# A hybrid encoder trunk: the rms factor applied late, D's heads rotated together, and two projections moved between scores

## The chip, the cores and the metric

The kernel runs on one core of one Trainium2 chip. The metric is device time in microseconds of that core. The core has TensorE (PE; its weight loads are shown as PEld), VectorE (DVE), ScalarE (ACT), GpSimd (POOL) and SyncE (SP), which issues the DMAs. Each engine runs its own list of instructions in order and waits on semaphores for the others.

## The reference

Two layers, each with three residual sub-layers, on 512 tokens of width 1024: a mixer of four parallel head groups, an attention to 256 memory tokens, and a dense squared-ReLU MLP. Queries and keys of every group are normalised per head by their root mean square; D's are then rotated.

```python
def rms(x, g):
    y = xf * lax.rsqrt(jnp.mean(xf * xf, axis=-1, keepdims=True) + EPS)
    return (y * g.astype(F32)).astype(x.dtype)

def axial_gqa(q, k, v, g_qk, row, col):          # group D; A, B and C likewise, with other heads and biases
    q = axial_rope(rms(q, g_qk[0]), row, col)
    k = axial_rope(rms(k, g_qk[1]), row, col)
    ...
        p = jax.nn.softmax(sc, axis=-1)

def memory_xattn(h, mem_n, w_xq, w_xkv, g_qk, w_xo):
    q = rms((h @ w_xq).reshape(b, s, X_HEADS, X_DH), g_qk[0])
    kv = (mem_n @ w_xkv).reshape(b, m, 2, X_HEADS, X_DH)
    ...
    return o.reshape(b, s, X_HEADS * X_DH) @ w_xo
```

The rms factor is one number per token and head. A gain is one number per channel, and a rotation mixes channels of one head, so the factor may be multiplied in before or after both.

## The kernel before

All 512 tokens stay on the chip; weights are streamed. Every product is made of float32r matmuls on a high and a low part: `mm3` (L176 to 180) issues three matmuls on the same PSUM tile, high x high (L177), and the two mixed ones (L178, L179). A weight tile is loaded by SP into `wst` (3 buffers), ACT casts it to the high part `whi` (L299, 4 buffers), and POOL subtracts to get the low part `wlo` in four pieces (L167 in `sub_lo`, 4 buffers).

The mixer runs twelve units, B 0 to 3, A 0 to 3, C 0 and 1, D 0 and 1. While the attention of one unit runs, the front of the next is computed: `front_A`, `front_G` (for C and D) and `front_B`. A front projects four token blocks of 128 (`tok_proj`), ACT copies and squares each result and DVE sums the squares (L415, into `sf`). Then `half(j)` works on two token blocks at a time: POOL adds epsilon and takes the power -1/2 (`rpow`, L311 and L312; in `front_B` L716 to 718), DVE multiplies queries and keys by that factor (L452, L552, L722), then by the gains (L454, L557, L725) and, in B and D, rotates them (`rope`, L584, L586, L587). ACT casts the high part and DVE subtracts for the low part (both into `spl`, 2 buffers), and PE transposes them (L403, into PSUM `dn`, 2 buffers), after which the copies `T` (L172 on ACT, L174 on DVE) feed the scores. In D, `rope` is called once for the four query heads and once for the key head; its scratch tile `zr` holds 512 columns, and each call makes four products of 16 columns per head, a product with the cosines and an addition.

Gate and branch products (`gate_piece`, `branch_piece`, PSUM `df`, one buffer) fill PE between the steps of the attentions, by the hand-written string `FILL`.

In the attention to the memory (`xattn`) a token block is projected (24 matmuls of 512 columns into `dn`) and normalised by `xnorm_split`; `q_trans(pr)` transposes the two blocks of pair `pr`, `attend(pr)` makes scores (PSUM `sc`, 2 buffers), softmax (L931 to L936), transposes (L941) and value products for two pairs of heads in turn, and `out_proj(pr)` multiplies by the output weights. The order in the code is projections 0 and 1, projections 2 and 3, `q_trans(0)`, `attend(0)` with `q_trans(1)` before its second half, `attend(1)`, `out_proj(0)`, `out_proj(1)`.

The order of each engine's instructions is made when the kernel is built: a list scheduler simulates the engines and issues, among the instructions whose inputs are there, the one that stands first in the program; `tc.high_priority()` puts an instruction ahead of the others. On the chip that order is fixed.

Of the kernel before, what the change touches and what calls it, by code (L numbers as in the profile page):

```python
# [11 lines left out]
F32R = mybir.dt.float32r  # L12
# [4 lines left out]
P = 128  # L17
# [76 lines left out]
def kernel(  # L94
# [214 lines left out]
    def rpow(dst, src, add, n):  # L309

        G.tensor_scalar(dst, src, add, None, op0=ALU.add)  # L311
        G.tensor_tensor(out=dst, in0=dst, in1=mhalf[:, :n], op=ALU.pow)  # L312

# [117 lines left out]
    def front_A(l, norm, h):  # L431
# [15 lines left out]
        def half(j):  # L447
# [3 lines left out]
            qq, kk = qk[:, :, 0:2, :], qk[:, :, 2:4, :]  # L451
            V.tensor_tensor(out=qk, in0=qk, in1=bc(s.rearrange("p (t h) -> p t h", t=2), 3, 64), op=ALU.mult)  # L452
            for m in range(2):
                V.tensor_tensor(out=kk[:, :, m], in0=kk[:, :, m], in1=bc(ga, 1, 2), op=ALU.mult)  # L454
            sq_ = tl("spl", [P, 2, 2, 2, 64], F32R)
            sk = tl("spl", [P, 2, 2, 2, 2, 64], F32R)
# [76 lines left out]
    def front_G(l, norm, br, g):  # L533
# [14 lines left out]
        def half(j):  # L548
            tk, s = toks[j], st[j]
            rpow(s, s, 64 * EPS, 10)  # L550
            qk = tk[:, :, :320].rearrange("p t (h d) -> p t h d", h=5)
            V.tensor_tensor(out=qk, in0=qk, in1=bc(s.rearrange("p (t h) -> p t h", t=2), 3, 64), op=ALU.mult)  # L552
            kk = qk[:, :, 4, :]
            if br == "C":
                V.tensor_tensor(out=kk, in0=kk, in1=bc(gc, 1, 2), op=ALU.mult)
            else:
                V.tensor_tensor(out=qk, in0=qk, in1=bc(gd, 1, 2), op=ALU.mult)  # L557
                rope(qk[:, :, 0:4], dt_, j, 4, 2)
                rope(qk[:, :, 4:5], dt_, j, 1, 2)
            sq_ = tl("spl", [P, 2, 4, 2, 64], F32R)  # L560
# [15 lines left out]
    def rope(x, tab, j, nh, nax):  # L576

        w = nax * 32
        b2 = slice(2 * j, 2 * j + 2)
        tmp = tl("zr", [P, S])[:, :2 * nh * w].rearrange("p (t h d) -> p t h d", t=2, h=nh)  # L580
# [111 lines left out]
    def front_B(l, cT, p):  # L692
# [20 lines left out]
        for j in range(2):  # L713
            tk, s = toks[j]
            s3 = s.rearrange("p (t c) -> p t c", t=2)
            G.tensor_scalar(s3[:, :, 0:4], s3[:, :, 0:4], 64 * EPS, None, op0=ALU.add)  # L716
            G.tensor_scalar(s3[:, :, 4:6], s3[:, :, 4:6], 32 * EPS, None, op0=ALU.add)
            G.tensor_tensor(out=s, in0=s, in1=mhalf[:, :12], op=ALU.pow)
            qr = tk[:, :, 0:64].rearrange("p t (h d) -> p t h d", h=2)
            qk = tk[:, :, 64:320].rearrange("p t (h d) -> p t h d", h=4)  # L720
            qn, kn = qk[:, :, 0:2], qk[:, :, 2:4]
            V.tensor_tensor(out=qk, in0=qk, in1=bc(s3[:, :, 0:4], 3, 64), op=ALU.mult)  # L722
            V.tensor_tensor(out=qr, in0=qr, in1=bc(s3[:, :, 4:6], 3, 32), op=ALU.mult)
            for h in range(2):
                V.tensor_tensor(out=kn[:, :, h], in0=kn[:, :, h], in1=bc(gbn, 1, 2), op=ALU.mult)  # L725
            for t_ in range(2):
                V.tensor_tensor(out=qr[:, t_], in0=qr[:, t_], in1=bc(gqr, 1, 2), op=ALU.mult)
            rope(qr, bt_, j, 2, 1)
            sq_ = tl("spl", [P, 2, 2, 2, 96], F32R)
            sk = tl("spl", [P, 2, 2, 2, 96], F32R)  # L730
# [89 lines left out]
    def mem_prep(l):  # L820
# [3 lines left out]
        for c in range(2):  # L824
            st = tl("wst", [P, 4, NM])
            SY.dma_start(st, memT[c * 512:(c + 1) * 512, :].rearrange("(k p) t -> p k t", p=P))
            for k in range(4):
# [8 lines left out]
                else:  # L836
                    q = tl("zr", [P, S])[:, :NM]
                    A.activation(q, st[:, k, :], AF.Square)
# [60 lines left out]
    def xattn(l, norm, KT, VX, X, nm):  # L899
# [6 lines left out]

        def proj(pr):
            tok_proj(norm, views, S, ev, tbs=(2 * pr, 2 * pr + 1))

# [6 lines left out]

        def attend(pr):
            for hp in range(2):
                if hp == 1 and pr == 0:
                    q_trans(1)  # L920
                pth = tl("pt", [P, 2, 2, 256], F32R)
                ptl = tl("pt", [P, 2, 2, 256], F32R)
                for qi in range(2):
                    Tq = Tqs[2 * pr + qi]
                    ps = psum("sc").rearrange("p (h k) -> p h k", h=2)
                    for i in range(2):
                        h = 2 * hp + i
                        hs = slice(h * P, (h + 1) * P)
                        mm3(ps[:, i], Tq[:, 0, hs], Tq[:, 1, hs], KT[0][:, h, :], KT[1][:, h, :], True, True)
                    st = stat(6)  # L930
                    V.tensor_reduce(out=st[:, 0:2], in_=ps, axis=AX.X, op=ALU.max, negate=True)  # L931
                    e = ptile()[:, :S].rearrange("p (h k) -> p h k", h=2)
                    for i in range(2):
                        A.activation(e[:, i], ps[:, i], AF.Exp, bias=st[:, i:i + 1], accum_out=st[:, 2 + i:3 + i])
                    V.reciprocal(st[:, 4:6], st[:, 2:4])
                    V.tensor_tensor(out=e, in0=e, in1=bc(st[:, 4:6], 2, NM), op=ALU.mult)  # L936
                    qs = slice(qi * P, qi * P + P)
                    pt = psum("tr")
                    for i in range(2):
                        for kb in range(2):  # L940
                            T.transpose(pt[:, (2 * i + kb) * P:(2 * i + kb + 1) * P], e[:, i, kb * P:(kb + 1) * P], idf)  # L941
                    pv_ = pt.rearrange("p (k q) -> p k q", k=4)
                    hi = pth[:, :, :, qs].rearrange("p h k q -> p (h k) q")
                    lo = ptl[:, :, :, qs].rearrange("p h k q -> p (h k) q")
                    A.copy(hi, pv_)
                    V.tensor_tensor(out=lo, in0=pv_, in1=f(hi), op=ALU.subtract)
                po = psum("pv").rearrange("p (h q) -> p h q", h=2)
                for i in range(2):
                    h = 2 * hp + i
                    for kb in range(2):  # L950
                        hs = slice(h * P, (h + 1) * P)
                        mm3(po[:, i], VX[0][:, kb, hs], VX[1][:, kb, hs], pth[:, i, kb, :], ptl[:, i, kb, :], kb == 0,
                            kb == 1)
                for i in range(2):
                    h = 2 * hp + i
                    ds_ = slice(pr * 256, pr * 256 + 256)
                    A.copy(xo[h][:, 0, ds_], po[:, i])
                    V.tensor_tensor(out=xo[h][:, 1, ds_], in0=po[:, i], in1=f(xo[h][:, 0, ds_]), op=ALU.subtract)

# [15 lines left out]

        proj(0)
        proj(1)
        q_trans(0)
        attend(0)
        attend(1)  # L980
        out_proj(0)
# [294 lines left out]
```

## Time and profile before

| | |
|---|---|
| median of 3 runs | 2363.65 us (2363.37 to 2367.36) |
| the profiled execution | 2361.96 us, of which the span from first to last instruction is 2360.0 us |
| mean granted PE clock | 0.992 of 2.4 GHz |
| busy, share of the span | PE 97%, DVE 59%, POOL 55%, ACT 49% |
| chain of work that ended last | PE 83%, DVE 11%, POOL 2% |

The share of busy time says which engine is nearest to its limit; the waits say which engine made another idle, and for how long in total, how often and at most; the timeline says what ran at a given moment. Ends of matmuls are modelled by the profiler, so they overlap a little.

### The profile page before, as it was taken

The numbers are of one execution on the slowest core, as the hardware profiler recorded it, in microseconds if no ns is written. First come the engines' busy times: TensorE is split into PE (matmuls) and PEld (weight loads), VectorE is DVE, ScalarE is ACT, GpSimd is POOL, SyncE is SP. The second block draws the span as 40 slices with busy tenths as digits, with TensorE's granted clock in tenths as the row PEclk, the third lists the DMA queues.
The fourth block names the chain that finished last, engine by engine and source line by source line (L and its number), as shares of the span: only waits on it lengthen the run. The fifth ranks groups of instructions, "written<-read, shape, count | busy, mean of one in ns | idle before, by whom it ended". The sixth has DMA issues, their size and how long they took to land.

```text
span 2360.0 us, 33643 instructions
## 1 busy us (share of the span) xinstructions
PE 2281.5 (97%) x12032; PEld 1966.0 (83%) x12032; DVE 1384.1 (59%) x2980; ACT 1151.8 (49%) x2253; POOL 1299.0 (55%) x1657
## 2 busy tenths in 40 slices
PE   8999999998999899999999998999989999999999
PEld 7888889887888888888888887898878878888887
DVE  7778666888975642222457786568879648222222
ACT  4556556655653543223345565566556546322321
POOL 7553544625465376666665435355353754766663
PEclk9999999999999999999999999999999999999999
DMA  5321342442454133333343214324425531323332
GB/s 185 108 94 57 102 138 66 127 154 84 147 179 155 54 99 98 98 92 96 111 134 101 83 46 127 113 79 134 136 92 168 171 131 56 106 91 97 98 93 77
DMA packets 88775, 258.25 MB, mean 109 GB/s; under 512 B 9704, under 2 KB 12392, under 8 KB 88608
## 3 DMA queue, kind: packets, MB, share of 16 engines
q1 hardware_dynamic: 88608, 256.10, 34.4%
q8 instruction: 95, 1.56, 0.3%
q14 instruction: 72, 0.59, 0.1%
HBM read 222.46 MB, written 33.60 MB: 109 GB/s over the span
## 4 chain that ended last, share of the span: by engine, by line
PE 83%; DVE 11%; POOL 2%; issue 1%; ACT 1%; DMA 1%; SPq 0%; POOLq 0%; ACTq 0%; DVEq 0%
PE dn L177 13%; PE dn L178 13%; PE dn L179 13%; PE df L177 10%; PE df L179 9%; PE df L178 9%; PE tr L476 3%; PE sc L177 1%; PE sc L179 1%; PE sc L178 1%; PE dn L403 1%; POOL wlo L167 1%; DVE pt L480 1%; DVE zr L584 1%; PE sc L624 1%
## 5 line engine op out<-in xcount | busy, mean ns | idle before, releaser
L167 POOL TENSOR_TENSOR wlo<-wst,whi 128x256 fp32r<-128x256 f32 (+3 forms) x1400 | 1071.0, 797 | 745.4 <-ACT whi L299 671.3
L299 ACT CAST whi<-wst 128x1024 fp32r<-128x1024 f32 (+3 forms) x350 | 348.8, 1003 | 640.8 <-PE dn L178 293.7
L177 PE MATMUL df<-s,whi 128*128 128x512 f32 (+1 forms) x967 | 381.0, 394 | 8.1 <-DVE zg L785 3.2
L179 PE MATMUL df<-s,wlo 128*128 128x512 f32 (+1 forms) x967 | 376.1, 389 | 1.3 <-POOL wlo L167 1.3
L178 PE MATMUL df<-s,whi 128*128 128x512 f32 (+1 forms) x967 | 374.3, 387 | 1.6 <-DVE s L167 1.6
L177 PE MATMUL dn<-whi,s 128*128 128x384 f32 (+4 forms) x768 | 264.8, 348 | 13.6 <-ACT s L348 7.7
L179 PE MATMUL dn<-whi,s 128*128 128x384 f32 (+4 forms) x768 | 263.3, 343 | 0.0
L178 PE MATMUL dn<-wlo,s 128*128 128x384 f32 (+4 forms) x768 | 263.1, 344 | 0.0
L177 PEld LDWEIGHTS df<-s,whi 128*128 128x128 f32 x967 | 181.7, 188 | 46.6 <-DVE yl L808 6.1
L179 PEld LDWEIGHTS df<-s,wlo 128*128 128x128 f32 x967 | 181.8, 188 | 38.4 <-POOL wlo L167 2.9
L178 PEld LDWEIGHTS df<-s,whi 128*128 128x128 f32 x967 | 181.9, 188 | 34.3 <-DVE s L167 2.2
L178 PE MATMUL dn<-s,whi 128*128 128x512 f32 (+1 forms) x529 | 197.1, 373 | 0.0
L179 PE MATMUL dn<-s,wlo 128*128 128x512 f32 (+1 forms) x529 | 196.9, 373 | 0.0
L177 PE MATMUL dn<-s,whi 128*128 128x512 f32 (+1 forms) x529 | 196.5, 374 | 0.0
L177 PEld LDWEIGHTS dn<-whi,s 128*128 128x128 f32 x768 | 146.8, 192 | 24.5 <-ACT s L348 7.7
L480 DVE TENSOR_TENSOR pt<-tr,pt 128x512 fp32r<-128x512 f32 (+1 forms) x224 | 142.7, 644 | 26.0 <-ACT pt L479 17.3
L178 PEld LDWEIGHTS dn<-wlo,s 128*128 128x128 f32 x768 | 147.2, 192 | 8.9 <-POOL wlo L167 0.2
L179 PEld LDWEIGHTS dn<-whi,s 128*128 128x128 f32 x768 | 146.8, 191 | 6.9
L479 ACT CAST pt<-tr 128x512 fp32r<-128x512 f32 (+1 forms) x224 | 121.8, 556 | 55.9 <-PE tr L476 54.3
L311 POOL TENSOR_SCALAR sf<-sf 128x8 f32<-128x8 f32 (+2 forms) x44 | 13.9, 316 | 241.3 <-DVE sf L415 239.5
L179 PEld LDWEIGHTS dn<-s,wlo 128*128 128x128 f32 x529 | 99.6, 188 | 17.9 <-POOL wlo L167 0.2
L178 PEld LDWEIGHTS dn<-s,whi 128*128 128x128 f32 x529 | 99.6, 188 | 17.8
(376 smaller groups left out, 4827.3 us busy)
## 6 DMA issues: line engine op xcount, KB each, us to landing
wst<-in_wts_dram SPq DMA_DIRECT2D x272, 512.0 KB, 3.5
wst<-in_wts_dram SPq DMA_DIRECT2D x64, 384.0 KB, 3.1
yl<-yz SPq DMA_DIRECT2D x48, 512.0 KB, 4.0
yz<-zg SPq DMA_DIRECT2D x64, 256.0 KB, 2.2
yz<-yl SPq DMA_DIRECT2D x48, 256.0 KB, 3.0
bias<-tscr SPq DMA_DIRECT2D x16, 320.0 KB, 3.3
yl<-yz SPq DMA_DIRECT2D x16, 256.0 KB, 3.1
bias<-tscr SPq DMA_DIRECT2D x8, 448.0 KB, 3.5
```

The costliest lines, as they stand in the source:

```text
L167: (eng or V).tensor_tensor(out=dst, in0=src, in1=f(hi), op=ALU.subtract)
L177: a = T.matmul(ps, lhsT=lh, rhs=rh, start=first, stop=False)
L178: T.matmul(ps, lhsT=lh, rhs=rl, start=False, stop=False)
L179: b = T.matmul(ps, lhsT=ll, rhs=rh, start=False, stop=last)
L299: chain("wh", A.copy(hi[:, :n], st[:, :n]))
L311: G.tensor_scalar(dst, src, add, None, op0=ALU.add)
L403: T.transpose(ps[:rows_, i * P:(i + 1) * P], s, idn)
L476: T.transpose(ps[:, kb * P:(kb + 1) * P], src[:, kb * P:(kb + 1) * P], idn)
L479: A.copy(hi, pv)
L480: V.tensor_tensor(out=lo, in0=pv, in1=f(hi), op=ALU.subtract)
L584: V.tensor_tensor(out=tmp[:, :, :, o:o + 16], in0=x[:, :, :, oo:oo + 16], in1=bc(tab[:, 1, b2, o:o + 16], 2, nh), op=ALU.mult)
L624: T.matmul(ps[:, :nk], lhsT=q, rhs=Tk[:, 0, kb0 * P:kb0 * P + nk], start=True, stop=False)
```

## The change

`rpow` adds epsilon on DVE instead of POOL and gives the power a high priority; `front_B` does the same in its own lines. In `front_A`, `front_G` and `front_B` the multiplication by the factor moves behind the gains and the rotation. In D one call of `rope` rotates five heads, with a scratch tile of 640 columns. In `xattn` projections 2 and 3 move behind the first and the second half of the first pair's attention, one at a time, and use the PSUM buffer `df`; `attend` is split by pairs of heads.

```diff
     def rpow(dst, src, add, n):
-        G.tensor_scalar(dst, src, add, None, op0=ALU.add)
-        G.tensor_tensor(out=dst, in0=dst, in1=mhalf[:, :n], op=ALU.pow)
+        V.tensor_scalar(dst, src, add, None, op0=ALU.add)
+        with tc.high_priority():
+            G.tensor_tensor(out=dst, in0=dst, in1=mhalf[:, :n], op=ALU.pow)
...
             rpow(s, s, 64 * EPS, 8)
-            V.tensor_tensor(out=qk, in0=qk, in1=bc(s.rearrange("p (t h) -> p t h", t=2), 3, 64), op=ALU.mult)
             for m in range(2):
                 V.tensor_tensor(out=kk[:, :, m], in0=kk[:, :, m], in1=bc(ga, 1, 2), op=ALU.mult)
+            V.tensor_tensor(out=qk, in0=qk, in1=bc(s.rearrange("p (t h) -> p t h", t=2), 3, 64), op=ALU.mult)
...
-            rpow(s, s, 64 * EPS, 10)
-            V.tensor_tensor(out=qk, in0=qk, in1=bc(s.rearrange("p (t h) -> p t h", t=2), 3, 64), op=ALU.mult)
             if br == "C":
                 V.tensor_tensor(out=kk, in0=kk, in1=bc(gc, 1, 2), op=ALU.mult)
             else:
                 V.tensor_tensor(out=qk, in0=qk, in1=bc(gd, 1, 2), op=ALU.mult)
-                rope(qk[:, :, 0:4], dt_, j, 4, 2)
-                rope(qk[:, :, 4:5], dt_, j, 1, 2)
+                rope(qk, dt_, j, 5, 2)
+            rpow(s, s, 64 * EPS, 10)
+            V.tensor_tensor(out=qk, in0=qk, in1=bc(s.rearrange("p (t h) -> p t h", t=2), 3, 64), op=ALU.mult)
...
-            G.tensor_scalar(s3[:, :, 0:4], s3[:, :, 0:4], 64 * EPS, None, op0=ALU.add)
-            G.tensor_scalar(s3[:, :, 4:6], s3[:, :, 4:6], 32 * EPS, None, op0=ALU.add)
-            G.tensor_tensor(out=s, in0=s, in1=mhalf[:, :12], op=ALU.pow)
+            V.tensor_scalar(s3[:, :, 0:4], s3[:, :, 0:4], 64 * EPS, None, op0=ALU.add)
+            V.tensor_scalar(s3[:, :, 4:6], s3[:, :, 4:6], 32 * EPS, None, op0=ALU.add)
+            with tc.high_priority():
+                G.tensor_tensor(out=s, in0=s, in1=mhalf[:, :12], op=ALU.pow)
...
-            V.tensor_tensor(out=qk, in0=qk, in1=bc(s3[:, :, 0:4], 3, 64), op=ALU.mult)
-            V.tensor_tensor(out=qr, in0=qr, in1=bc(s3[:, :, 4:6], 3, 32), op=ALU.mult)
...
             rope(qr, bt_, j, 2, 1)
+            V.tensor_tensor(out=qk, in0=qk, in1=bc(s3[:, :, 0:4], 3, 64), op=ALU.mult)
+            V.tensor_tensor(out=qr, in0=qr, in1=bc(s3[:, :, 4:6], 3, 32), op=ALU.mult)
...
-        def proj(pr):
-            tok_proj(norm, views, S, ev, tbs=(2 * pr, 2 * pr + 1))
+        def proj(*tbs):
+            tok_proj(norm, views, S, ev, tbs=tbs, tags=("dn", "dn", "df", "df"))
...
-        proj(0)
-        proj(1)
+
+        proj(0, 1)
         q_trans(0)
-        attend(0)
-        attend(1)
+        attend(0, 0)
+        proj(2)
+        attend(0, 1)
+        proj(3)
+        q_trans(1)
+        attend(1, 0)
+        attend(1, 1)
         out_proj(0)
         out_proj(1)
```

## Rows read from the trace of the kernel before

**Rows 1.** The page, first part: busy us (share of the span) and instructions of each engine.

```profile
PE 2281.5 (97%) x12032; PEld 1966.0 (83%) x12032; DVE 1384.1 (59%) x2980; ACT 1151.8 (49%) x2253; POOL 1299.0 (55%) x1657
```

**Rows 2.** Waits of PE: who waited for whom, us in total, times, longest.

```profile
PE dn L403 <- DVE spl L167: 18.9, 7, 5.4
...
PE sc L177 <- ACT p L934: 6.1, 2, 3.1
PE dn L177 <- DVE sf L415: 4.0, 3, 1.6
...
PE dn L403 <- ACT spl L732: 2.8, 3, 1.1
PE pv L177 <- ACT pt L945: 2.4, 2, 1.2
```

**Rows 3.** Timeline, A, layer 0: start, us, instruction, [idle before <- releaser].

```profile
287.40 0.42 DVE L415 TENSOR_REDUCE sf<-dn 128x4 f32<-128x256 f32 x1 [0.51 <-ACT dn L413]
...
293.20 1.67 POOL L312 TENSOR_TENSOR sf<-sf,mhalf 128x8 f32<-128x8 f32 x1
...
295.07 0.90 DVE L452 TENSOR_TENSOR tok<-tok,sf 128x512 f32<-128x512 f32 x1
...
298.20 0.72 PE L403 MATMUL dn<-jr,spl 128*128 128x128 f32 x4 [3.83 <-DVE spl L167]
```

**Rows 4.** Timeline, D's second half, layer 0.

```profile
537.29 0.47 DVE L415 TENSOR_REDUCE sf<-dn 128x5 f32<-128x320 f32 x1
...
538.46 2.28 POOL L167 TENSOR_TENSOR wlo<-wst,whi 128x192 fp32r<-128x192 f32 x4
540.71 1.98 POOL L312 TENSOR_TENSOR sf<-sf,mhalf 128x10 f32<-128x10 f32 x1
...
542.72 1.22 DVE L552 TENSOR_TENSOR tok<-tok,sf 128x640 f32<-128x640 f32 x1 [1.81 <-POOL sf L312]
...
545.11 1.59 DVE L584 TENSOR_TENSOR zr<-tok,ropd_t 128x128 f32<-128x128 f32 x4
...
549.22 0.84 DVE L584 TENSOR_TENSOR zr<-tok,ropd_t 128x32 f32<-128x32 f32 x4
...
551.65 1.23 PE L403 MATMUL dn<-idr,spl 128*128 128x128 f32 x8 [5.42 <-DVE spl L167]
```

**Rows 5.** Timeline, PE, layer 1: the stalls of A and of D's second half.

```profile
1471.15 0.72 PE L403 MATMUL dn<-jr,spl 128*128 128x128 f32 x4 [3.81 <-DVE spl L167]
...
1724.02 1.23 PE L403 MATMUL dn<-idr,spl 128*128 128x128 f32 x8 [3.88 <-DVE spl L167]
```

**Rows 6.** Windows over six half-clock stretches: length, each engine's busy us, PEclk, DMA; sum.

```profile
549.00:559.20 10.20, 7.04 (x28) 6.82 (x29) 5.17 (x13) 2.48 (x5) 0.70 (x2) 0.50 0.27 83
...
sum 37.40, PE 29.52 PEld 28.44 DVE 23.26 ACT 11.10 POOL 11.43; mean PE 4.92 PEld 4.74 DVE 3.88 ACT 1.85 POOL 1.91
```

**Rows 7.** Timeline, PE, memory attention, layer 0: third projection's start, first transposes.

```profile
773.39 0.50 PE L177 MATMUL dn<-whi,s 128*128 128x512 f32 x1 [1.60 <-DVE sf L415]
...
784.43 0.80 PE L403 MATMUL tr<-idr,spl 128*128 128x128 f32 x8
```

**Rows 8.** Timeline, D's first half, layer 0: a pow on POOL, and DVE.

```profile
521.25 1.99 POOL L312 TENSOR_TENSOR sf<-sf,mhalf 128x10 f32<-128x10 f32 x1
...
521.40 0.67 DVE L167 TENSOR_TENSOR s<-of,s 128x512 fp32r<-128x512 f32 x1
...
525.99 0.82 DVE L557 TENSOR_TENSOR tok<-tok,gd 128x640 f32<-128x640 f32 x1
```

**Rows 9.** Waits of POOL, ACT, DVE and PE around the weight split.

```profile
POOL wlo L167 <- ACT whi L299: 671.3, 219, 29.5
ACT whi L299 <- PE dn L178: 293.7, 82, 4.6
...
DVE tok L722 <- POOL sf L718: 12.5, 6, 2.9
...
PE df L179 <- POOL wlo L167: 1.3, 2, 1.1
```

More of the change, by code (lines that the diff above doesn't have):

```diff
@@ L579, in rope @@
         b2 = slice(2 * j, 2 * j + 2)
-        tmp = tl("zr", [P, S])[:, :2 * nh * w].rearrange("p (t h d) -> p t h d", t=2, h=nh)
+        tmp = tl("zr", [P, 640])[:, :2 * nh * w].rearrange("p (t h d) -> p t h d", t=2, h=nh)
         for ax in range(nax):
@@ L836, in mem_prep @@
                 else:
-                    q = tl("zr", [P, S])[:, :NM]
+                    q = tl("zr", [P, 640])[:, :NM]
                     A.activation(q, st[:, k, :], AF.Square)
@@ L915, in q_trans @@
                 Tqs.append(Tq)
[L917 to L947, printed above, removed]
@@ L948, in attend @@
+        def attend(pr, hp):
+            pth = tl("pt", [P, 2, 2, 256], F32R)
+            ptl = tl("pt", [P, 2, 2, 256], F32R)
+            for qi in range(2):
+                Tq = Tqs[2 * pr + qi]
+                ps = psum("sc").rearrange("p (h k) -> p h k", h=2)
                 for i in range(2):
                     h = 2 * hp + i
-                    for kb in range(2):
-                        hs = slice(h * P, (h + 1) * P)
-                        mm3(po[:, i], VX[0][:, kb, hs], VX[1][:, kb, hs], pth[:, i, kb, :], ptl[:, i, kb, :], kb == 0,
-                            kb == 1)
@@ L954, in attend @@
[L954 to L958, printed above, removed]
+                    hs = slice(h * P, (h + 1) * P)
+                    mm3(ps[:, i], Tq[:, 0, hs], Tq[:, 1, hs], KT[0][:, h, :], KT[1][:, h, :], True, True)
+                st = stat(6)
+                V.tensor_reduce(out=st[:, 0:2], in_=ps, axis=AX.X, op=ALU.max, negate=True)
@@ new lines, in attend @@
+                e = ptile()[:, :S].rearrange("p (h k) -> p h k", h=2)
+                for i in range(2):
+                    A.activation(e[:, i], ps[:, i], AF.Exp, bias=st[:, i:i + 1], accum_out=st[:, 2 + i:3 + i])
+                V.reciprocal(st[:, 4:6], st[:, 2:4])
+                V.tensor_tensor(out=e, in0=e, in1=bc(st[:, 4:6], 2, NM), op=ALU.mult)
+                qs = slice(qi * P, qi * P + P)
+                pt = psum("tr")
+                for i in range(2):
+                    for kb in range(2):
+                        T.transpose(pt[:, (2 * i + kb) * P:(2 * i + kb + 1) * P], e[:, i, kb * P:(kb + 1) * P], idf)
@@ new lines, in attend @@
+                pv_ = pt.rearrange("p (k q) -> p k q", k=4)
+                hi = pth[:, :, :, qs].rearrange("p h k q -> p (h k) q")
+                lo = ptl[:, :, :, qs].rearrange("p h k q -> p (h k) q")
+                A.copy(hi, pv_)
+                V.tensor_tensor(out=lo, in0=pv_, in1=f(hi), op=ALU.subtract)
+            po = psum("pv").rearrange("p (h q) -> p h q", h=2)
+            for i in range(2):
+                h = 2 * hp + i
+                for kb in range(2):
+                    hs = slice(h * P, (h + 1) * P)
+                    mm3(po[:, i], VX[0][:, kb, hs], VX[1][:, kb, hs], pth[:, i, kb, :], ptl[:, i, kb, :], kb == 0,
+                        kb == 1)
@@ L960, in xattn @@
+            for i in range(2):
+                h = 2 * hp + i
+                ds_ = slice(pr * 256, pr * 256 + 256)
+                A.copy(xo[h][:, 0, ds_], po[:, i])
+                V.tensor_tensor(out=xo[h][:, 1, ds_], in0=po[:, i], in1=f(xo[h][:, 0, ds_]), op=ALU.subtract)
         w = []
```

## The prediction

> **What bounds the kernel now.** I read three views in turn. The page's first part says that TensorE (PE) is busy for 97% of the span, with every other engine at 59% or less [rows 1]. So the only time to win is what PE loses: 2360.0 - 2281.5 = 78.5 us of idle time, plus what it works at the lower clock. The list of PE's waits says where the idle time lies [rows 2]: 18.9 us in seven stalls of the fronts' transposes (L403) behind the last subtraction on VectorE (DVE), 2.8 us of the same line behind ScalarE (ACT) in front_B, and in the attention to the memory 6.1 us behind the exponentials (L934) and most of 4.0 us behind the squared sums (L415), which hold PSUM buffers. The rest is scattered over waits that the change does not touch. The timeline then shows what stands behind each stall.
>
> In head group A [rows 3] the squared sums are ready at 287.40 + 0.42 = 287.82, but the pow on GpSimd (POOL) starts at 293.20, behind pieces of the weight split (wlo); DVE can only multiply by the factor at 295.07, and then come the gains (L454), the casts and the subtractions. PE has run dry at 298.20 - 3.83 = 294.37. The second layer repeats it with 3.81 us [rows 5]. In D's second half [rows 4] the sums are ready at 537.76, four wlo pieces go first, the pow ends at 542.69, DVE has idled 1.81 us, and PE stands for 5.42 us until 551.65. In the second layer the same stall is 3.88 us [rows 5].
>
> A long stall costs twice. The stretches of half clock (1.2 of 2.4 GHz) in mid-span are six: the two A stalls, the two D stalls and the two memory attentions, each with such a stall at its start. They last 37.4 us together, and PE is busy for 29.52 us in them [rows 6]. Work at half clock takes twice as long, so 14.8 us are lost, 3.5 of them (half of 7.04) in D of the first layer and 2.3 on average in each of the other five. The Trainium skill (TensorE: Matmul & The Clock Gate, Terms) prices throttled time at the time times one minus the granted ratio, which would be 18.7 us; the rows show that PE is idle for part of it, and the rows decide. By the page the sum below would gain some 3 us more.
>
> **The change, part by part.**
> *A: late factor and early pow.* The add goes to DVE; bounded by nothing and the 0.42 us of the reduce before it, since it writes eight numbers per partition. A high-priority pow waits for at most the piece that is running, 2.28/4 = 0.57 us [rows 4], and takes 1.67 [rows 3]. It is ready by 287.82 + 0.42 + 0.57 + 1.67 = 290.5, while the gains run beside it. The multiplication takes 0.90 us, until 291.4. Between its end in the kernel before (295.97) and PE's start (298.20) lie 2.23 us, some of them gain products that now come earlier; so the transposes are ready by 293.6 at the latest, before PE runs dry at 294.37. Both long stalls go: 3.83 + 3.81 = 7.6 us. Three short ones make up 18.9 - 7.64 - 5.42 - 3.88 = 2.0 us; I take 1.5.
>
> *D: the same, and one rotation in place of two.* Today four q heads and then the k head are rotated separately, with six DVE instructions each; after it there are six for both. Those on 128 elements take 1.59/4 = 0.40 us, those on 32 take 0.84/4 = 0.21 [rows 4], so by a straight line one on 160 takes 0.46. The path from the sums to PE loses 1.81 us of idle time and the 0.84 us of small products, and gets 4 x 0.06 = 0.25 us for the wider products, some 0.5 for two full-width steps at 640 in place of 512 elements (a quarter of 0.82 to 1.22 us each, rows 4 and the quiet one in [rows 8]), and up to 0.4 for the add: 1.5 to 1.9 us shorter. The first half's rotation, which stands ahead on the same queue, is shorter too, by nothing to twice the 0.84 (its products ran beside wlo). So PE's stall of 5.42 falls by 1.5 to 3.6 us, and that of 3.88 as much: I take 3.2 and 3.0 (nearer the upper end, since the first half's six products beside wlo weigh more than those of the second), 6.2 us, and a remainder of 2.2 and 0.9.
>
> *B.* Its 2.8 us are the same chain (reduce, add, pow, multiply, gains, rotation); I take 1.5, bounds 0 and 2.8. The pow also moves past wlo pieces on POOL: 68 pows (48 of front halves, 20 others) go ahead of weight splits. I cost that at nothing, because POOL itself waits 671.3 us for ACT's casts and PE waits for wlo only 1.3 us in all [rows 9]; without that cover each would cost up to its own length.
>
> *Memory attention.* Today all four projections come first: the third waits 1.60 us for a PSUM buffer [rows 7], and after the fourth nothing is left to fill the softmax, so PE stands up to 3.1 and then 1.2 us: with 6.1, 2.4 [rows 2] and twice 1.60 [rows 7] that is 11.7 us in both layers. Now the third goes to the buffer df, which nothing else holds there, so the 1.60 us go. A projection is (784.43 - 773.39)/2 = 5.5 us of PE work; the third covers the normalisation of the first two, the fourth the first softmax. What is late next: df is one buffer, so the fourth must wait until ACT and DVE have emptied the third, two ACT passes and a reduction; and after the fourth the last block's chain must be bridged by the output projection. Bounds for what is left: 0 to the present 5.8 a layer; I take 1.8, which is a stall like the 1.60 and a little. Gain 8.0 us.
>
> *Clock.* If no stall above some 2 us is left in these places, the half clock goes with them: up to 14.8 us. The stall of 1.60 us at 773.39 [rows 7] is followed by none of the six stretches; the stalls that were are 3 us and longer, the shortest of them up to 3.1 [rows 2]. D's remainder of 2.2 us lies between, so I take back 12.5.
>
> **Sum:** 7.6 + 1.5 + 6.2 + 1.5 + 8.0 + 12.5 = 37.3 us. The profiled execution took 2361.96 us (span 2360.0 and 1.96 around it); less 37.3 is 2324.7. It stood 1.7 us below the median of the runs, 2363.65, so the forecast is 2326 us, 1.6% less.
>
> **Does an early pow slow DVE?** In [rows 8] a pow runs from 521.25 to 523.24, and inside it a DVE subtraction with two SBUF inputs takes 0.67 us for 512 elements, 1.31 ns each; with POOL idle the 640-wide product takes 0.82, 1.28 ns each. So it does not, while beside wlo the same width takes 1.22 [rows 4]. The Trainium skill (SBUF — State Buffer, SBUF: two separate sides) says the opposite for this change: a DVE instruction with two SBUF inputs and a GpSimd instruction that reads SBUF exclude each other, and the later one blocks for the whole length of the other. This trace disagrees for the pow; if the page held, the pow would hide under nothing, and that is the third rival.
>
> **The rivals.**
> *1. The memory attention starves.* The query weights stay in their four wlo buffers until the fourth projection, so the output weights (2.28 us on POOL for a tile of 768 columns [rows 4], so 3.0 for one of 1024) come later, and PE finds nothing to fill with. For it: rings of four, and ACT's casts wait 293.7 us for PE to free them. Against: today's fourth projection ends at 784.43, and a shift of some 5 us meets weights that are split at the pace at which two output columns use them. Then 8.0 and some 3 us of clock do not come: 2337; with 5 us of new stalls a layer 2347.
> *2. D stays late.* The casts or PSUM copies are next on its path: 6.2 and 5 us less, 2337; with rival 1 together 2348.
> *3. The pow blocks DVE.* The gains and rotations wait for it, the front's path is as long as before, and only the memory attention and the removal of wlo pieces ahead of the pow are left: some 14 us, 2350. It would be within 0.2% if the attention starves too. Against it stands the row of 0.67 us.
> *4. Slower.* The factor product comes last on DVE's in-order queue. If the pow is held by a wlo piece that waits for ACT's cast, which waits for PE to free a buffer, then DVE stands with everything behind it, among it the subtractions of the running attention, which PE needs. DVE waits today 12.5 us in 6 places for such a pow in front_B [rows 9]. There are 48 front halves; the gains and this balance at 37.3/48 = 0.8 us for each, and at 1.0 us it is 2374. It needs POOL to be late on average; that POOL idles 671.3 us speaks against it.
>
> **Chances.** Forecast 0.60 (own range 2310 to 2338), rival 1 0.14, rival 2 0.11, rival 3 0.07, rival 4 0.08. The low end is all that the touched places lose: 18.9 + 2.8 + 11.7 + 14.8 = 48.2 us, with 4 us for short stalls elsewhere that shift: 2310. The high end takes in both rivals that keep part of the gain, 2348. Left out are rival 4, half of rival 3 and 0.05 of the forecast. A measurement here tells about 0.2%, 4.7 us, from no change. Faster by more: 0.60 + 0.13 + 0.10 + 0.03 = 0.86; within: 0.01 + 0.01 + 0.04 = 0.06; slower 0.08.
>
> **What would show it.** The L403 stalls behind DVE fall from 18.9 to below 5 us; no A stall is left; the pow starts within 1 us of its add; L552 and its like no longer wait for POOL; the D half has one group of 160-wide products; the scores of the memory attention are followed by L177 on df and no stall of 3 us; the granted clock is full from the first microseconds to the last. The forecast is wrong if half-clock stretches stay while the stalls shrink, if new PE waits for wlo appear, or if DVE waits for the pow at its late place.

## The result and the profile after

The changed kernel takes 2340.65 us in the median of four runs (2338.06 to 2346.09), the kernel before on the same chip 2365.51 us (four runs): a ratio of 0.9898 [0.9876, 0.9919], 1.0% less. The profiled execution took 2338.06 us (span 2336.1), against 2361.96: 23.9 us less, where the forecast had taken off 37.3. The sign is right, and the time lies inside the range of 2310 to 2348, though 2.65 us above the 2338 up to which the forecast reckoned by itself: it lies in the part that was added for rivals. 13.4 us of the sum did not come. The question is which of its terms those were.

The page of after, first part, and its list of PE's waits (who waited for whom, us in total, times, longest):

```profile
PE 2273.1 (97%) x12032; PEld 1958.0 (84%) x12032; DVE 1396.7 (60%) x3016; ACT 1145.7 (49%) x2253; POOL 1285.4 (55%) x1573
```

```profile
PE df L177 <- DVE zg L786: 8.5, 12, 2.1
...
PE pv L648 <- DVE pt L481: 4.0, 5, 1.4
...
PE tr L404 <- ACT spl L896: 3.7, 2, 1.9
...
PE sc L177 <- ACT p L932: 1.8, 2, 0.9
...
PE dn L404 <- DVE spl L167: 1.0, 1, 1.0
```

Lines have moved by one to three: L404 is L403 of before, L932 is L934. What led [rows 2] is gone: the transposes' wait for the subtraction on DVE fell from 18.9 us to 1.0, and the scores' wait for the exponentials from 6.1 to 1.8. New are 3.7 us of transposes behind ACT's cast (L896), which is in the attention to the memory, and small waits behind DVE in the mixers.

The windows of before and of after, cut at the first matmul of each query projection and at the start of the next layer, tell which stage gained. Columns: window, length, then busy us of PE, PEld, DVE, ACT and POOL, granted PE clock, DMA share, GB/s. The four rows are the mixer of layer 0, its attention to the memory with the MLP behind it, and the same two of layer 1. Before:

```profile
0.00:759.00 759.00, 722.47 (x4022) 633.67 (x4023) 556.68 (x1279) 429.37 (x897) 395.00 (x525) 0.99 0.39 123
759.00:1196.73 437.73, 430.12 (x2040) 358.31 (x2039) 158.94 (x241) 160.62 (x254) 276.93 (x328) 1.00 0.32 96
1196.73:1926.80 730.07, 706.97 (x3971) 622.91 (x3970) 527.42 (x1237) 415.67 (x873) 368.98 (x493) 0.99 0.36 116
1926.80:2360.00 433.20, 421.94 (x2003) 351.15 (x2001) 141.04 (x223) 146.12 (x232) 258.12 (x313) 0.99 0.28 89
```

After:

```profile
0.00:742.76 742.76, 716.63 (x4022) 629.67 (x4023) 557.05 (x1295) 427.77 (x898) 387.78 (x486) 1.00 0.39 125
742.76:1181.97 439.21, 432.51 (x2041) 359.50 (x2039) 158.25 (x243) 159.46 (x253) 275.17 (x325) 0.99 0.32 96
1181.97:1902.20 720.23, 700.77 (x3970) 617.58 (x3969) 538.62 (x1251) 412.83 (x873) 364.31 (x455) 1.00 0.37 117
1902.20:2336.10 433.90, 423.18 (x2003) 351.27 (x2001) 142.74 (x227) 145.60 (x232) 258.19 (x309) 1.00 0.29 89
```

The mixers became 16.2 and 9.8 us shorter, 26.1 together (unrounded). The attention with the MLP became 1.5 and 0.7 us longer. By this table the fronts gave everything, and the moved projections, on which 8.0 us and a share of the clock had been counted, gave nothing. It compares one execution of each kernel; the first two runs below settle it.

Why they gave nothing stands in the timeline of after, layer 0 (start, us, instruction, [idle before <- releaser]; first ACT's casts and PE's idle time, then the order of PE around them):

```profile
760.23 0.69 ACT L413 ACTIVATE tok<-df,r_x 128x512 f32<-128x512 f32 x1 [1.46 <-PE df L179]
760.82 0.65 ACT L414 ACTIVATE df<-df,r_x 128x512 f32<-128x512 f32 x1
...
761.39 1.27 ACT L896 CAST spl<-tok 128x512 fp32r<-128x512 f32 x2
...
762.06 0.54 PE L404 MATMUL tr<-idr,spl 128*128 128x128 f32 x4 [1.86 <-ACT spl L896]
762.61 0.50 PE L177 MATMUL df<-whi,s 128*128 128x512 f32 x1
...
773.91 0.39 PE L177 MATMUL sc<-T,T 128*128 128x256 f32 x1 [0.91 <-ACT p L932]
775.66 0.63 PE L939 MATMUL tr<-idr,p 128*128 128x128 f32 x4 [0.76 <-DVE p L934]
...
778.36 0.39 PE L177 MATMUL pv<-pt,T 128*128 128x256 f32 x1 [0.68 <-ACT pt L943]
...
780.07 0.38 PE L178 MATMUL pv<-pt,T 128*128 128x256 f32 x1 [1.33 <-DVE pt L944]
```

The third projection (on `df`) was already over at 760.2, before the first transposes: in the built order of PE its matmuls alternate with those of the first two. ACT copies and squares it ahead of the first block's cast, and PE stands 1.86 us. The fourth starts at 762.61, ahead of the scores: 21 of its 24 matmuls precede the first of them. When the softmax comes, nothing is left to fill it, and the stall of up to 3.1 us of before [rows 2], with the shorter one behind it, has become four short ones. The text of the program has the projections between the scores; the order that the list scheduler wrote down has them ahead of them. By the scheduler's rule that is so because `df` was free and their inputs were there; no run tried the same order without `df`.

### The profile page after: what moved, and what is told of

Read it like the earlier page. It is cut to its first block, busy times and chain, and to the rows that moved or that the text cites. A ratio compares the mean times of both kernels' runs of the same rounds, so it can differ in the third digit from the quotient of the medians.

```text
span 2336.1 us, 33596 instructions
## 1 busy us (share of the span) xinstructions
PE 2273.1 (97%) x12032; PEld 1958.0 (84%) x12032; DVE 1396.7 (60%) x3016; ACT 1145.7 (49%) x2253; POOL 1285.4 (55%) x1573
## 3 DMA queue, kind: packets, MB, share of 16 engines
q8 instruction: 95, 1.56, 0.3%
## 4 chain that ended last, share of the span: by engine, by line
PE 85%; DVE 10%; issue 2%; POOL 2%; ACT 1%; DMA 0%; SPq 0%; DVEq 0%; ACTq 0%; POOLq 0%
PE dn L177 13%; PE dn L178 13%; PE dn L179 13%; PE df L177 10%; PE df L178 10%; PE df L179 10%; PE tr L477 3%; POOL wlo L167 1%; PE dn L404 1%; PE sc L177 1%; DVE pt L481 1%; PE sc L179 1%; PE sc L178 1%; DVE spl L167 1%; PE pv L648 1%
## 5 line engine op out<-in xcount | busy, mean ns | idle before, releaser
L167 POOL TENSOR_TENSOR wlo<-wst,whi 128x256 fp32r<-128x256 f32 (+3 forms) x1400 | 1084.3, 808 | 715.0 <-ACT whi L299 629.0
L177 PE MATMUL dn<-whi,s 128*128 128x384 f32 (+4 forms) x736 | 249.4, 344 | 9.8 <-ACT s L349 7.8
L178 PE MATMUL dn<-wlo,s 128*128 128x384 f32 (+4 forms) x736 | 250.2, 340 | 0.0
L179 PE MATMUL dn<-whi,s 128*128 128x384 f32 (+4 forms) x736 | 250.0, 340 | 0.0
L313 POOL TENSOR_TENSOR sf<-sf,mhalf 128x8 f32<-128x8 f32 (+2 forms) x44 | 73.7, 1675 | 220.3 <-DVE sf L311 205.3
L177 PEld LDWEIGHTS dn<-whi,s 128*128 128x128 f32 x736 | 138.9, 190 | 19.5 <-ACT s L349 7.8
L178 PEld LDWEIGHTS dn<-wlo,s 128*128 128x128 f32 x736 | 139.4, 189 | 7.7
L179 PEld LDWEIGHTS dn<-whi,s 128*128 128x128 f32 x736 | 139.3, 189 | 5.3
L178 PEld LDWEIGHTS dn<-s,whi 128*128 128x128 f32 x529 | 99.5, 188 | 18.3 <-DVE s L956 0.5
L177 PEld LDWEIGHTS dn<-s,whi 128*128 128x128 f32 x529 | 98.6, 188 | 18.9 <-DVE T L876 0.4
```

Of the source, the lines that this page charges most:

```text
L167: (eng or V).tensor_tensor(out=dst, in0=src, in1=f(hi), op=ALU.subtract)
L177: a = T.matmul(ps, lhsT=lh, rhs=rh, start=first, stop=False)
L178: T.matmul(ps, lhsT=lh, rhs=rl, start=False, stop=False)
L179: b = T.matmul(ps, lhsT=ll, rhs=rh, start=False, stop=last)
```

## The experiments

Each ran beside the kernel before on the same chip. "Fronts" below is the changed kernel with the attention to the memory as before.

**One part at a time.** The fronts alone:

```diff
-            tok_proj(norm, views, S, ev, tbs=tbs, tags=("dn", "dn", "df", "df"))
+            tok_proj(norm, views, S, ev, tbs=(2 * pr, 2 * pr + 1))
...
-        proj(0, 1)
+        proj(0)
+        proj(1)
         q_trans(0)
-        attend(0, 0)
-        proj(2)
...
+        attend(0)
+        attend(1)
```

> The changed kernel with the memory attention of before; the fronts (late factor, early pow, one rotation in D) as changed. Theory (the fronts carry the whole gain, since the stage of the memory attention took 92.7 and 90.7 us after, against 90.8 and 89.1 before): 22 to 27 us below before, that is 2338 to 2343, no slower than the changed kernel, with the waits of 3.1, 1.6 and 1.2 us in the memory attention back. Rival (the memory attention gave its 8 to 11 us and the fronts fell short): 14 us below before, about 2351.

Measured: 2339.33 us (2337.43 to 2341.12), ratio 0.9885 [0.987, 0.99]. The waits of the memory attention are back where they were, the longest 2.77 us for the exponentials, and the time is that of the whole change, as the theory said.

The memory attention alone, with the fronts of before, so in the kernel before:

```diff
-            tok_proj(norm, views, S, ev, tbs=(2 * pr, 2 * pr + 1))
+            tok_proj(norm, views, S, ev, tbs=tbs, tags=("dn", "dn", "df", "df"))
...
-        attend(0)
-        attend(1)
+        attend(0, 0)
+        proj(2)
+        attend(0, 1)
+        proj(3)
```

> The kernel before with the memory attention of the changed kernel alone. Theory (as it is issued, the third projection runs inside the first two and 21 of the 24 matmuls of the fourth ahead of all scores, so no softmax is filled): within 4 us of before. Rival (the new order fills the softmax): 8 to 11 us below before.

Measured: 2364.86 us, ratio 0.9993 [0.9984, 1.0002]: nothing that can be measured. The two runs agree with the stage table.

**Holding the projections.** If the order is at fault, it can be written out. An ordering edge without a semaphore keeps the first matmul of a projection behind a chosen PE instruction; in the first variant the fourth stands behind the second block's first scores (`held`):

```diff
-                mm3(ps[:, :width], t[:, 0, sl], t[:, 1, sl], hi[:, k % 2, :], lo[:, k % 2, :], k == 0, k == KD - 1)
+                i = mm3(ps[:, :width], t[:, 0, sl], t[:, 1, sl], hi[:, k % 2, :], lo[:, k % 2, :], k == 0, k == KD - 1)
+                if behind is not None and k == 0:
+                    tc.add_manual_dep(i[0].ins, behind.ins.name, ...)
...
         attend(0, 0)
+        held = last_sc[0]
         proj(2)
         attend(0, 1)
-        proj(3)
+        proj(3, behind=held)
```

> The changed kernel with the first matmul of the fourth projection ordered behind the second block's first scores, on the same engine and so without a semaphore; 23 of its 24 matmuls then stand between the two pairs of scores. Theory (filler was spent too early): PE's waits for the softmax in the memory attention (L932 to L944, some 4 us a layer in the changed kernel) fall below 1.5 us a layer, the total 2 to 6 us below the changed kernel, 2335 to 2339. Rival (normalisation and softmax are a chain that no order shortens): the waits move to the transposes and the scores, and the total stays within 2 us of the changed kernel.

Measured: 2339.88 us, ratio 0.9887 [0.9872, 0.9902], no gain over the changed kernel. Its order has 23 of the fourth's 24 matmuls between the scores, as wanted, but PE's idle time there only moved (timeline, PE, layer 0):

```profile
763.74 0.53 PE L407 MATMUL tr<-idr,spl 128*128 128x128 f32 x4 [1.86 <-ACT spl L899]
764.98 1.23 PE L407 MATMUL tr<-idr,spl 128*128 128x128 f32 x8 [0.71 <-DVE sf L311]
...
781.05 0.50 PE L177 MATMUL dn<-s,whi 128*128 128x256 f32 x2 [1.21 <-ACT s L959]
```

The 1.86 us at the start are untouched: they belong to the third. So the third was held too, behind the last matmul of the second:

```diff
         proj(0, 1)
+        first = last_mm[0]
         q_trans(0)
         attend(0, 0)
         held = last_sc[0]
-        proj(2)
+        proj(2, behind=first)
         attend(0, 1)
         proj(3, behind=held)
```

> As x_hold3, and the third projection ordered behind the last matmul of the second, so that it covers the normalisation of the first two blocks and the fourth covers the first softmax, which is what the prediction reckoned with. Theory: PE's idle time in the stage is 2 us a layer or less, no stretch of half clock is left there, and the total is 8 to 11 us below fronts_only, about 2330. Rival (chain that no order shortens): within 2 us of the changed kernel.

Measured: 2330.28 us (2326.31 to 2331.93), ratio 0.9844 [0.983, 0.9858]. The interval lies clear of the changed kernel's [0.9876, 0.9919]: this version is 10 us faster than it by the medians (13 by the ratios) and 37 us faster than the kernel before, the best that was run. PE's idle time in the memory attention of layer 0, and then the windows of its two attentions with their MLPs:

```profile
763.04 0.51 PE L410 MATMUL tr<-idr,spl 128*128 128x128 f32 x4 [0.16 <-DVE spl L167]
764.48 0.85 PE L410 MATMUL tr<-idr,spl 128*128 128x128 f32 x8 [0.92 <-DVE T L174]
...
776.66 0.39 PE L178 MATMUL pv<-pt,T 128*128 128x256 f32 x1 [1.56 <-DVE pt L951]
```

```profile
744.96:1177.73 432.77, 429.71 (x2041) 358.08 (x2040) 159.02 (x243) 158.62 (x253) 274.79 (x325) 1.00 0.32 97
...
1898.51:2328.10 429.59, 422.01 (x2003) 350.92 (x2001) 142.47 (x227) 144.96 (x232) 256.09 (x309) 0.99 0.28 90
```

PE idles 2.9 us there instead of 6.6, and the two stages are 6.4 and 4.3 us shorter than after's. The total came as the theory said; idle time of 2 us or less and no stretch of half clock, which it also named, did not (a stretch follows the 1.56 us in both layers).

Does the third's hold do this by itself? It alone:

```diff
         proj(2, behind=first)
         attend(0, 1)
-        proj(3, behind=held)
+        proj(3)
```

> The changed kernel with one hold only: the third projection stands behind the second on TensorE, the fourth is free and so takes most of its 24 product groups between the first block's first and second scores, the rest after the second block's. Theory (the third, spent too early between the first two, is what the change lost, and with it the fourth falls by itself among the scores): 2329 to 2334 us, the 9 to 10 us that the kernel with both holds gained over the changed kernel, or nearly all of it; PE idles 2.5 to 4 us in the attention to the memory of a layer. Rival (both projections must be held, one alone only moves the waits, as the hold of the fourth alone did): 2337 to 2342 us, with PE idle 5 to 7 us there.

Measured: 2337.53 us, ratio 0.9886 [0.9871, 0.9901]. In time the rival was right: as little as the fourth's hold alone. With the fourth free, 17 of its matmuls stand between the scores of the first two blocks, four behind the second's and three later, so the normalisation is covered (1.86 us became 0.17) but the softmax is not (timeline, PE, layer 0):

```profile
766.68 0.51 PE L410 MATMUL tr<-idr,spl 128*128 128x128 f32 x4 [0.17 <-DVE spl L167]
...
778.62 0.63 PE L946 MATMUL tr<-idr,p 128*128 128x128 f32 x4 [0.80 <-DVE p L941]
781.20 1.08 PE L946 MATMUL tr<-idr,p 128*128 128x128 f32 x4 [1.95 <-ACT p L939]
```

The last variant puts both holds into the kernel with the memory attention alone, so behind the old fronts:

```diff
-        proj(2)
+        proj(2, behind=first)
         attend(0, 1)
-        proj(3)
+        proj(3, behind=held)
```

> The kernel before with the change of the attention to the memory alone, both later projections held in their written order on TensorE; fronts as before. Theory (the two parts add up: the held order is worth some 9 us whatever the fronts do): 2354 to 2359 us, ratio 0.995 to 0.9975. Rival (the order of the attention helps only once the fronts' stalls are gone, since before them the time is lost or found elsewhere): 2362 to 2368 us, no difference that can be measured from the kernel before.

Measured: 2365.79 us (11 runs), ratio 0.9995 [0.9986, 1.0004]. The theory that the two parts add up fell. In the profiled execution the two attentions with their MLPs are 2.2 and 1.7 us shorter than before's, but the mixers 2.3 and 5.6 us longer; D's stall in layer 0 is 6.51 us there, against 5.42 [rows 4]. Up to the attention of layer 0 PE's built order is that of the kernel before, so the 2.3 us are no effect of the edit on that order; whether the 5.6 of layer 1 are one isn't settled by one profile. Before's profile, besides, is one of its fastest executions, 5.6 us below the median beside this run (2367.56). Nor is this all: the attentions with their MLPs gain only 3.9 us here and 10.4 behind the new fronts (432.77 and 429.59 against 437.86 and 434.88 in "fronts"). What holds is the measured sum: the held order is worth 10 us behind the new fronts and nothing that can be measured behind the old. Why is open.

**The parts of the fronts.** The three edits of the fronts were undone one at a time, in the kernel "fronts". First two rotations again:

```diff
-                rope(qk, dt_, j, 5, 2)
+                rope(qk[:, :, 0:4], dt_, j, 4, 2)
+                rope(qk[:, :, 4:5], dt_, j, 1, 2)
```

> fronts_only with D's heads rotated in two calls again, four query heads and the key head. Theory (DVE stands on D's path, so the 0.84 us of small products and the two narrow steps come back there twice a layer): D's stall of the transposes behind DVE comes back with 1.5 to 3 us a layer, and with it up to 3.5 us of half clock; 3 to 8 us above fronts_only, 2342 to 2347. Rival (with the factor late and the pow early there is room on DVE): within 2 us of fronts_only, 2339.

Measured: 2346.6 us, ratio 0.9919 [0.9907, 0.9931]: one rotation instead of two is worth some 8 us (0.9919 - 0.9885 = 0.0034 of 2366), at the upper end of the theory's range. Its path is shown only in part. Behind the subtraction on DVE D's transposes wait 1.15 us, in layer 0 alone, and the gate product of layer 1's D waits 3.01 us in place of 2.08; the half-clock stretches of layer 0 in its profile (at 294.6, 465.3 and 581.3) have their like in another execution of "fronts" (the last run below, at 293.2, 463.9 and 580.0), so they don't tell of the rotation. Then the factor early again, with the add on DVE and the pow's priority kept:

```diff
+            V.tensor_tensor(out=qk, in0=qk, in1=bc(s.rearrange("p (t h) -> p t h", t=2), 3, 64), op=ALU.mult)
             for m in range(2):
                 V.tensor_tensor(out=kk[:, :, m], in0=kk[:, :, m], in1=bc(ga, 1, 2), op=ALU.mult)
-            V.tensor_tensor(out=qk, in0=qk, in1=bc(s.rearrange("p (t h) -> p t h", t=2), 3, 64), op=ALU.mult)
```

(and likewise in `front_G` and `front_B`)

> fronts_only with the factor multiplied first again, before the gains and the rotation, in A, B, C and D; add on DVE, high priority of the pow and the single rotation stay. Theory (the pow's place in POOL's queue is what cost the time; in A it is ready 3 us before it was, which is enough by itself): the A stalls stay away, D's come back in part, 2 to 8 us above fronts_only, 2341 to 2347. Rival (the late factor is what counts, since it hides the whole pow): both A and D stalls come back, with their half clock, 12 to 20 us above, 2351 to 2359.

Measured: 2367.84 us, ratio 1.0009 [0.9999, 1.0019]. Without the late factor nothing is left of the gain: the theory fell. The rival named the cause, but its 12 to 20 us were too few for the 28 by the medians. The transposes wait 16.1 us for the subtraction again, in six places, the longest 5.2. Timeline of this kernel, A in layer 0:

```profile
289.28 1.63 POOL L313 TENSOR_TENSOR sf<-sf,mhalf 128x8 f32<-128x8 f32 x1
...
290.89 5.01 POOL L167 TENSOR_TENSOR wlo<-wst,whi 128x192 fp32r<-128x192 f32 x8
...
290.94 2.76 DVE L453 TENSOR_TENSOR tok<-tok,sf 128x512 f32<-128x512 f32 x1 [0.98 <-POOL sf L313]
...
294.23 1.22 DVE L455 TENSOR_TENSOR tok<-tok,ga 128x128 f32<-128x128 f32 x2
...
296.33 0.72 PE L404 MATMUL dn<-jr,spl 128*128 128x128 f32 x4 [3.19 <-DVE spl L167]
```

The pow is done 4 us earlier than in [rows 3] (290.91 against 294.87), yet the transposes still wait 3.19 us, since gains and casts all stand behind the factor and the factor's product takes 2.76 us beside `wlo`. Then the pow without priority and the add on POOL again, the factor late:

```diff
-        V.tensor_scalar(dst, src, add, None, op0=ALU.add)
-        with tc.high_priority():
-            G.tensor_tensor(out=dst, in0=dst, in1=mhalf[:, :n], op=ALU.pow)
+        G.tensor_scalar(dst, src, add, None, op0=ALU.add)
+        G.tensor_tensor(out=dst, in0=dst, in1=mhalf[:, :n], op=ALU.pow)
```

(and likewise in `front_B`)

> fronts_only with the add on POOL again and no priority for the pow; late factor and single rotation stay. Theory (place in the queue counts): the A stalls come back with some 2.5 us each, as only the gains (1.2 us) are hidden, D's do not; with half clock 5 to 12 us above fronts_only, 2344 to 2351. Rival (the late factor alone is enough): within 2 us of fronts_only.

Measured: 2347.85 us, ratio 0.9925 [0.9913, 0.9938], some 9 us, as the theory said. The A stall is back (3.14 us at 295.43, 1.81 in layer 1): the pow starts at 291.23, behind four pieces of `wlo` that start at 289.00. The run undoes the add's engine and the priority together; it doesn't tell them apart. Last, `rpow` ahead of gain and rotation in the program of C and D, meant to bring add and pow early there too:

```diff
             tk, s = toks[j], st[j]
+            rpow(s, s, 64 * EPS, 10)
...
-            rpow(s, s, 64 * EPS, 10)
```

> fronts_only with add and pow of C and D ahead of the gains and the rotation in the program, the multiplication still last. In the changed kernel's trace the add of D's second half stood on DVE behind the rotation, 3 us after its sums, and the pow 1.7 to 3.4 us after the add. Theory (this delay reaches PE in D of the second layer alone, where the gate product waits 2.1 us behind DVE): 0 to 4 us below fronts_only, DVE no longer waits 1.4 us for the pow there. Rival (the add, when early, only takes DVE's time from the running attention): 0 to 3 us above.

Measured: 2339.83 us, ratio 0.9889 [0.9874, 0.9903]: the same as "fronts". But it doesn't test the place of the add. Timeline of this kernel, D's second half in layer 0:

```profile
528.97 0.47 DVE L416 TENSOR_REDUCE sf<-dn 128x5 f32<-128x320 f32 x1
...
532.37 0.30 DVE L584 TENSOR_TENSOR zr<-tok,ropd_t 128x160 f32<-128x160 f32 x1
532.60 0.56 DVE L311 TENSOR_SCALAR sf<-sf 128x10 f32<-128x10 f32 x1
```

The add still stands behind the four products, 3.2 us after its sums. On PE, DVE, ACT and POOL alike the order of instructions, told by their tiles and shapes, is that of "fronts": the edit moved a line of the program and nothing on the chip. So what an early add in D is worth stays open, and the run is a second sample of "fronts". It shows how far two executions of one order differ: the profiled ones took 2338.94 and 2343.08 us, with PE busy at half clock for 16.8 and 26.6 us.

The parts do not add up. By the ratios 8, 29 and 9 us are lost when one is undone, some 46 in all, of a joint gain of 27. Each shortens the same chain to the transposes. Without the late factor the other two gave nothing; without one of the other two 18 to 19 us were left.

## Why the prediction was right, and where it failed

**The fronts: right, the sum in part by luck.** The mixers gave 26.1 us. The sum had 7.6 + 1.5 + 6.2 + 1.5 = 16.8 us for them and, of the 14.8 us lost at half clock, 14.8 - 2 x 2.3 = 10.2 outside the memory attentions, less the 2.3 withheld for D: 24.7 in all. L403's waits for the subtraction on DVE fell from 18.9 to 1.0 us (below 5 was asked), and those for ACT in front_B from 2.8 to 0.7: 20.0 us, where 15.3 and 1.5 were forecast. Waits that the sum had at nothing took some of it back (small waits, below), so that the totals agree to 1.4 us is in part chance. Both rivals that let the fronts fail, D staying late and the blocked DVE, are refuted.

**A: right in the end, wrong in its steps.** The forecast had the pow start at most 0.57 us after the add, then the factor's product, and PE without a stall. Timeline of after, A in layer 0:

```profile
282.71 4.62 POOL L167 TENSOR_TENSOR wlo<-wst,whi 128x192 fp32r<-128x192 f32 x8
...
283.72 0.92 DVE L454 TENSOR_TENSOR tok<-tok,ga 128x128 f32<-128x128 f32 x2 [0.17 <-ACT tok L413]
...
285.01 0.17 DVE L311 TENSOR_SCALAR sf<-sf 128x8 f32<-128x8 f32 x1
...
287.28 1.64 POOL L313 TENSOR_TENSOR sf<-sf,mhalf 128x8 f32<-128x8 f32 x1
...
288.95 1.07 DVE L455 TENSOR_TENSOR tok<-tok,sf 128x512 f32<-128x512 f32 x1 [1.10 <-POOL sf L313]
...
292.03 0.51 PE L404 MATMUL dn<-jr,spl 128*128 128x128 f32 x4 [1.04 <-DVE spl L167]
```

The add ends at 285.18 and the pow starts 2.1 us later, behind several pieces of `wlo`, not one: the priority orders the list when it is built, and the chip's order is then fixed, whatever is late. DVE waits 1.10 us for the pow at its late place and PE 1.04. "No A stall is left" and "within 1 us of its add" were wrong, at a price of 1 us in place of 3.83. The gains ran even before the sums, not beside the pow. Saving the rest took both edits: with the pow in its old place the stall is 3.14 us, with the factor ahead of the gains 3.19.

**D: more than forecast, by another road.** The second half in layer 0, timeline of after:

```profile
528.17 1.87 DVE L584 TENSOR_TENSOR zr<-tok,ropd_t 128x160 f32<-128x160 f32 x3
...
530.44 0.30 DVE L584 TENSOR_TENSOR zr<-tok,ropd_t 128x160 f32<-128x160 f32 x1
...
530.67 0.56 DVE L311 TENSOR_SCALAR sf<-sf 128x10 f32<-128x10 f32 x1
...
532.93 1.96 POOL L313 TENSOR_TENSOR sf<-sf,mhalf 128x10 f32<-128x10 f32 x1
533.09 0.80 DVE L587 TENSOR_TENSOR tok<-tok,zr 128x640 f32<-128x640 f32 x1
...
534.92 1.21 DVE L559 TENSOR_TENSOR tok<-tok,sf 128x640 f32<-128x640 f32 x1
...
540.27 0.51 PE L404 MATMUL dn<-idr,spl 128*128 128x128 f32 x4 [0.53 <-DVE T L174]
```

One group of 160-wide products, as predicted. The working had the add at once behind the sums. It stands behind the four products, 3 us after the sums, and the pow another 1.7 us behind it; with `rpow` ahead of the rotation in the program it stood there too, so why the scheduler put it there is open. PE's stall is nevertheless gone (0.53 us in layer 0 and 0.59 in layer 1, behind a copy `T`, where remainders of 2.2 and 0.9 were allowed). Undoing the one rotation costs 8 us, more than the few tenths that the products were given; of these the trace of that run shows the 1.15 us behind the subtraction and 0.9 more behind the gate at D, and the rest isn't traced.

**Does the pow block DVE?** The rotation's addition of 0.80 us at 533.09 lies wholly inside the pow, and costs what a quiet product of that width costs (0.82, [rows 8]). So rival 3 had no mechanism in the pow. What does hold up DVE is `wlo`: in after the gain product of D (L556) takes 0.81 us four times with POOL idle and 1.35 to 1.36 four times beside `wlo`. The factor's product of the run without the late factor, beside eight pieces of it, took 2.76, against 0.67 to 0.69 us for quiet two-input steps of that width. The Trainium skill (SBUF — State Buffer, SBUF: two separate sides) states an exclusive lock between a DVE instruction with two SBUF inputs and any GpSimd instruction that reads SBUF; the traces agree for `wlo` (1.36 against 0.81 us) and disagree for the pow (0.80 us).

**Memory attention: the step that failed.** The term was 8.0 us; measured are -2.2 (1.5 + 0.7 us longer). The step that failed starts at "the third goes to the buffer df, which nothing else holds there". That was true, and by the scheduler's rule it was the fault: a free buffer lets it issue the projection as soon as its inputs are there. "The third covers the normalisation of the first two, the fourth the first softmax" read the program's text as PE's order. With both held to that order the gain over "fronts" is 10 us in the runs (0.9844 against 0.9885) and 5.1 and 5.3 us in the two stages' windows (432.77 and 429.59 against 437.86 and 434.88), the 8.0 and part of its clock. The size was about right and the premise wrong. Rival 1 had this outcome (2337, without the 8.0 and some 3 us of clock) but another mechanism, late output weights; PE waited for `wlo` 0.2 us in all, against 1.3 before [rows 9], so it was not that.

**Clock: too high.** Four half-clock stretches are left in after, three of them in the memory attentions:

```profile
510.70:514.10 3.40, 3.40 (x11) 3.40 (x12) 3.40 (x13) 2.12 (x7) 0.00 (x0) 0.50 0.00 0
763.30:766.70 3.40, 3.40 (x10) 2.61 (x9) 1.22 (x2) 1.04 (x1) 1.93 (x2) 0.50 0.02 5
780.40:783.80 3.40, 3.40 (x18) 3.40 (x17) 1.91 (x5) 0.74 (x2) 0.00 (x0) 0.50 0.58 154
1937.50:1940.90 3.40, 3.40 (x16) 3.40 (x17) 3.07 (x5) 0.43 (x2) 2.27 (x2) 0.50 0.15 10
sum 13.60, PE 13.60 PEld 12.81 DVE 9.59 ACT 4.33 POOL 4.20; mean PE 3.40 PEld 3.20 DVE 2.40 ACT 1.08 POOL 1.05
```

PE is busy at half clock for 13.6 us instead of 29.5 [rows 6], so 6.8 us are lost instead of 14.8: 8.0 came back in these two executions, not 12.5. The argument was that single stalls of 1.6 us are followed by no such stretch. The stretch at 763.3 follows a stall of 1.86 us, that at 780.4 four stalls of 0.7 to 1.3 us one behind the other; with both holds one follows a single stall of 1.56 us (776.66: the matmuls behind it take 0.41 us, those of the scores before it 0.28). So the length of the single stall was no safe bound, and cutting one stall into four did not save the clock here. That the four together are the cause was not tried by itself. Nor is a stall's length alone a rule: the stall of 1.86 us in layer 1 of after (1921.50) is followed by no such stretch, and A's two stalls of 1.04 and 0.68 us in layer 0, alike in seven kernels with the new fronts, are followed by one in four of the seven profiles. How much of the clock comes back thus differs from execution to execution, by 4.9 us between the two of one order (half of 26.6 - 16.8).

**Small waits.** The list of after has 8.5 us behind `zg` (3.2 in before) and 4.0 behind `pt` (0.5). The longest, 2.1 us in layer 1's D, stands behind the rotation on DVE's queue (L586 and L587, 1690.74 to 1692.68); the others were not followed one by one. Rival 4, DVE held at its late place by a pow that POOL reaches late, exists (in layer 1's D, DVE waits 1.38 us for it), and with half-clock stretches that stay it is the second of the prediction's own signs of being wrong that came. But DVE waits for the fronts' pows 12.5 us in all, against 15.8 before: a few tenths per front half and not 1.0.

**The account.** Forecast against measured, from the profiled executions: fronts with their clock about 24.7 and 26.1; memory attention with its clock and the MLP behind it about 12.6 (8.0 + 2 x 2.3) and -2.2. (The 2.3 is the prediction's average; the two memory stretches of before, PE busy for 3.13 and 3.41 us, had lost 1.6 and 1.7, which moves 1.3 us from this term to the fronts.) 37.3 - 23.9 = 13.4 us is what the attention withheld (14.8), less what the fronts gave beyond their share (1.4).

## What to carry to other kernels

Where a list scheduler orders an engine, a step written between two others stands there only if something holds it: before counting filler against a wait, ask what keeps that filler from being spent earlier, and take a freed buffer as a likely reason that it will be. After an edit of the program's order look in the trace whether the engines' order moved at all. Apply a factor that comes late as the last product of its chain; the steps before it then cover its latency even if it is late itself. And undo the parts one at a time before adding them up: two holds that each gave nothing gave 10 us together, and three edits of one chain lost some 46 us singly of a joint 27.

## What the runs showed of the hardware beyond the forecast

A GpSimd pow on 128x10 elements (1.96 us) ran beside a two-input DVE addition of 640 elements at the quiet price (0.80 us), while wide two-input subtractions on GpSimd stretched a DVE product of 640 from 0.81 to 1.36 us and one of 512, at the worst place shown here, from some 0.7 to 2.76 us. And a granted clock of 0.50 followed stalls of 1.56 and 1.86 us, and four of 0.7 to 1.3 us in a row, while none followed the one of 1.60 us [rows 7] nor a second one of 1.86 us: a like stall was followed by half clock at one time and not at another.
